# Inverses of a gated DeltaNet layer in eight rows of products, and weight casts placed behind the layer's first norms

## The chip, the cores and the metric

The kernel runs on one core of a Trainium2 chip. The metric is the device time of one execution in microseconds; the time before is the median of three runs. The profile is of one execution, taken by the hardware profiler. TensorE (PE) does the matrix products and loads its weights beside them (PEld); VectorE (DVE), ScalarE (ACT) and GpSimd (POOL) do the rest; SyncE (SP) issues most transfers.

## The reference

A trunk of two residual layers works on 512 tokens of width 1024. Layer 0 mixes tokens by gated linear attention, layer 1 by a gated DeltaNet, and a gated ConvFFN follows each; every sublayer ends in a LayerNorm. What the change touches lies in layer 1:

```python
# DeltaNet, in chunks, per head
m = where(strict, einsum('bhnik,bhnjk->bhnij', k_beta, k) * decay_ij, 0.0)
rhs = concatenate([v * beta, k_beta * exp(bcum)], -1)
sol = triangular_solve(m, rhs, lower=True, unit_diagonal=True)
u, w = split(sol)
# then a scan over the chunks: v_new = u - w @ state; o = (q*exp(bcum)) @ state + qk @ v_new; ...
y = (rms_norm(o) * silu(gate)) @ w_out
h = layer_norm(ALPHA * h + y, ln_g[i, 0], ln_b[i, 0])
# ConvFFN
g, up = split(causal_dwconv(h @ w_in, conv_w))
h = layer_norm(ALPHA * h + (gelu(g) * up) @ w_out, ...)
```

Instead of the solve, the kernel forms the inverse of the unit triangular matrix, for eight heads and four chunks of 128 tokens.

## The kernel before

All wide products are done in three terms: each operand is split into a high part (a cast by ScalarE) and the rest (a subtraction by VectorE), both at reduced precision (`split_out`, L728), and high by high, high by low and low by high are summed in PSUM. Weights come in tiles of 128x1024: a load on SP's queue into one of three raw buffers (`RAWB`), then the cast `wh` and the subtraction `wl` into one of four pairs (`WB`). `prefetch` issues these tiles ahead of their use, in the order of a plan that is written beforehand (`plan_fm` for feature tiles, `plan_tm`, `plan_fold` and `plan_gated` for the others); `look` says how many tiles ahead, and `held` counts those that hold a pair.

The order of the work is written by a small planner in Python: `clk` is its estimate of PE's time, `spawn` starts a side task after a delay, `flags` say when something will be ready, and `pump` lets the side tasks whose time has come emit their instructions between two stretches of wide products. The tile framework then schedules these instructions by their order and its own estimates. Up to the first mixer's input products the order of PE is pinned (`keep_in_program_order`); from there on it isn't (`self.pin = False`). `behind(a, b)` adds an edge that keeps a behind b in the schedule.

**The inverses** (`inverses` in `gdn`). Blocks of 32x32 are inverted on VectorE (`base`) and reach PE's operands by DRAM: `rm` is the inverse that is being filled, `T` (`t8`) holds its diagonal blocks transposed, `am` is the matrix itself. Two heads make a pair, so there are four pairs. The doubling from 32 to 64 (`quarter(k)`) and from 64 to 128 (`half(k)`) has two products each: V = am times T, copied from PSUM, and then R from V and rm, copied into `rm`. A step k does the V of pair k and the R of pair k-1, for the eight (head, chunk) units of the pair. There are ten steps, five of each kind. Before each, `block_turn(INV_APART)` waits for its time and places the first product of the row behind the last 512-column product. Full inverses set the flag `("rm", head)`, for which the chains over the chunks (`chain(0)` for heads 0 to 3, `chain(1)` for 4 to 7) wait. Meanwhile PE works on the last feature tiles of the input products (`fm`) and on the gate's products (`gated`, tile name `fold`), which hold four PSUM banks of eight.

**The output projection and the norm** (`mixer_out`, `out_proj`, `ln`). The output is made in two halves of 512 columns. For the second half (`last`) all eight 128x512 weight pieces wait in slots (`wsh`, `wsl`), and the four token blocks of 128 are done one after the other: products, update of the residual `h` (L625), statistics (L632), and `ln` is spawned for the block. Its first part aggregates the statistics (L880), takes the root, and normalises the two halves of the block: ScalarE one (L903), VectorE the other (L904). Its second part transposes them on PE (`xT`, L234), applies gain and bias on ScalarE (L917), and splits them into the operand `xh`, `xl` of the feed-forward (L921, L924, L925). A third part makes the residual on POOL (L941, L942). `look` is raised to 8 at the start of the second half, so the first four feature tiles of the feed-forward are issued there, before the first block's products. `fm_items` then takes the first four feature tiles for tokens 0 to 255 first, as soon as blocks 0 and 1 are there, and for the other tokens later.

Of the kernel before, what the change touches and what calls it, by code (L numbers as in the profile page):

```python
# [13 lines left out]
ALU = mybir.AluOpType  # L14
# [5 lines left out]
NC = D // P  # L20
# [31 lines left out]
RAWB = 3  # L52
WB = 4
LOOKAHEAD = 2
TAIL = 4
HEADSTART = 4
HALVES = {True: 3, False: 4}
# [21 lines left out]
class Trunk:  # L79
# [3 lines left out]
    def __init__(self, ctx, tc):  # L83
        self.tc = tc
        self.nc = nc = tc.nc
        self.n = 0
        ec = ctx.enter_context
        ap = ec(tc.tile_pool(name="acts", bufs=1))
        self.xh = ap.tile([P, NC, S], F32R, name="xh", tag="xh")
        self.xl = ap.tile([P, NC, S], F32R, name="xl", tag="xl")  # L90
        self.wp = ec(tc.tile_pool(name="wts", bufs=WB))
        self.hp = ec(tc.tile_pool(name="resid", bufs=2 * NTB))
        self.rp = ec(tc.tile_pool(name="raws", bufs=RAWB))
        self.cp = ec(tc.tile_pool(name="const", bufs=1))
        self.sp = ec(tc.tile_pool(name="small", bufs=4))
        self.pp = ec(tc.tile_pool(name="ps", bufs=8, space=bass.MemoryType.PSUM))
        self.dp = ec(tc.tile_pool(name="scratch", bufs=1, space=bass.MemoryType.DRAM))
        self.mp = None
        self.stage("gla", GLA_SLOTS)
        self.resets()  # L100
        self.ident = self.keep([P, P], "ident")
        ones = self.keep([P, 32], "one")
        self.one, self.warm, self.eps = (ones[:, i:i + 1] for i in range(3))
        nc.gpsimd.memset(ones, 1.0)
        make_identity(nc, self.ident)
        nc.gpsimd.memset(self.eps, LN_EPS)
        self.h = None
        self.plan = []
        self.issued = 0
        self.loaded = 0  # L110
        self.taken = 0
        self.held = 0
        self.look = 1
        self.pin = True
        self.ready = []
        self.dve = 0.0
        self.clk = 0.0
        self.tasks = []
        self.flags = {}
        self.tabled = None  # L120
        self.wide = None
        self.block = None
        self.traced = None
        self.spilled = False
        self.next_block = 0.0
        self.parts = []
        self.after = ()
        self.inverted = {}
        self.third = None
        self.first = None  # L130
        self.pieces = []
        self.late = []
# [346 lines left out]
    def prefetch(self):  # L479
        while self.issued < min(len(self.plan), self.taken + self.look):  # L480
            self.load_ahead(self.issued + 1)
            item = self.plan[self.issued]
            if self.held == WB and not self.in_slots(item):
                break
            if self.issued >= self.taken and self.flags.get(("split", *item[2:4]), 0.0) > self.clk:
                break
            self.ready.append(self.issue(item))
            self.issued += 1
        self.load_ahead(self.taken + self.look + AHEAD)
# [123 lines left out]
                else:  # L613
                    done(tb, ps[tb][piece], piece, blk(piece, S // m))

    def out_proj(self, a, n, first, final, pieces=1):

        nc = self.nc
        self.st = [None] * NTB
        for hf in range(2):  # L620
            def done(tb, ps, piece=None, cols=slice(0, S), hf=hf):
                h, ps = self.h[tb][hf][:, cols], ps[:, cols]
                if first:
                    self.wait(("h", tb, hf))
                    nc.vector.scalar_tensor_tensor(h, h, ALPHA, ps, ALU.mult, ALU.add)  # L625
                else:
                    nc.vector.tensor_add(h, h, ps)
                self.vec(0.7, self.clk + 0.4)
                if final is not None:
                    if hf == 0:  # L630
                        self.st[tb] = self.small([P, 1 + (pieces if tb == NTB - 1 else 1), 6], f"ln_st{pieces}")
                    nc.vector.bn_stats(self.st[tb][:, hf + (piece or 0), :], h)  # L632
                    self.vec(0.7)
                    if hf == 1 and piece in (None, pieces - 1):
                        self.spawn(final(tb))
                        self.pump()

            last = hf == 1 and final is not None
            if last:
                self.sqrt_table()  # L640
                self.look = TAIL + WB
            self.tm_half(a, n, TAIL if last else 1, done, last, pieces if last else 1)
        self.look = LOOKAHEAD


    def out_rows(self, a, n, final, pieces):
# [7 lines left out]
        for tb in range(NTB):  # L654
# [29 lines left out]
            self.pump()  # L684
        self.look = LOOKAHEAD

# [101 lines left out]
    def load_x(self, x):  # L788
# [34 lines left out]
        def arrive(i):  # L823
            self.opening(*self.x_part(i, 1))
            self.opening(*split(2 * i + 1))
            if i:
                self.look = 1
                self.prefetch()
                for tb in range(2, NTB):
                    for hf in range(2):  # L830
                        load(tb, hf)
                self.look = LOOKAHEAD
                self.prefetch()
# [60 lines left out]
    def ln(self, tb, spill=False):  # L894

        nc = self.nc
        li, h = self.li, self.h[tb]
        for hf in range(2):
            self.flags.pop(("h", tb, hf))
        mv, rs = self.ln_stats(tb)  # L900
        nb = self.small([P, 1], "ln_nb")
        nc.vector.scalar_tensor_tensor(nb, mv[:, 0:1], -1.0, rs, ALU.mult, ALU.mult)
        nc.scalar.activation(h[1], h[1], AF.Identity, bias=nb, scale=rs)  # L903
        nc.vector.tensor_scalar(h[0], h[0], mv[:, 0:1], rs, op0=ALU.subtract, op1=ALU.mult)  # L904
        ready = self.vec(0.65)
        yield ready - self.clk + 0.2
        for hf in range(2):
            ps = self.psum("xT")
            self.tr4(ps, h[hf])
            xf = self.slot("xf")  # L910
            for j in range(4):
                c = li * NC + 4 * hf + j
                if spill and hf and tb == NTB - 1:
                    nc.vector.tensor_scalar(xf[:, blk(j)], ps[:, blk(j)], self.lg[:, c:c + 1], self.lb[:, c:c + 1],
                                            op0=ALU.mult, op1=ALU.add)
                else:
                    nc.scalar.activation(xf[:, blk(j)], ps[:, blk(j)], AF.Identity,  # L917
                                         bias=self.lb[:, c:c + 1], scale=self.lg[:, c:c + 1])
            xs = (slice(None), slice(4 * hf, 4 * hf + 4), blk(tb))
            if hf == 0:  # L920
                nc.vector.tensor_copy(self.xh[xs], c4(xf))  # L921
                self.vec(0.42, self.clk + 1.8)
            else:
                nc.scalar.copy(self.xh[xs], c4(xf))  # L924
            nc.vector.tensor_sub(self.xl[xs], c4(xf), self.xh[xs])  # L925
            ready = self.vec(0.7, self.clk + (2.6 if hf else 0.0))
        self.set(("x", tb), max(0.1, ready - self.clk))
        yield 0.0

        self.spilled = spill  # L930
        if spill:
            for hf in range(2):
                nc.gpsimd.dma_start(self.hd[blk(tb), blk(hf, S)], h[hf])
            self.h[tb] = None
            return
        for i in range(NTB):
            yield from self.until(("x", i))
        yield RESID_DELAY + 10.0 * tb
        gb = self.ln_gb()
        for hf in range(2):  # L940
            nc.gpsimd.tensor_mul(h[hf], h[hf], gb[hf])  # L941
            nc.gpsimd.tensor_add(h[hf], h[hf], gb[2 + hf])  # L942
            self.set(("h", tb, hf))
            yield 5.0
# [153 lines left out]
    def folded(self, forms, first):  # L1098
# [25 lines left out]
        for name, _, form, at in FOLD:  # L1124
            f = FORMS.index(form) * 256
            for i in range(0, m, 2):
# [13 lines left out]
                self.spend()  # L1140
        self.look = LOOKAHEAD

# [114 lines left out]
    def gated(self, forms, tag, done, last):  # L1257
# [45 lines left out]
        for name, form, at in GATED:  # L1303
# [31 lines left out]
            if last:  # L1335
                forms.pop(form, None)
        self.look = LOOKAHEAD


    def gla_plan(self, w_in, w_out):  # L1340
# [6 lines left out]
        self.plan_gated(w_in, 2048)  # L1347
        self.plan_out(w_out, 0, NC, TAIL)

# [237 lines left out]
        self.gated(forms, "sg", gate_done, True)  # L1587
        self.mixer_out(y, li, g, b)

    def mixer_out(self, y, li, g, b, final=None):  # L1590
        self.ln_begin(li, g, b)

        def a(c, tb):
            hf = c // 4
            self.wait(("y", tb, hf))
            return tuple(t[:, blk(c % 4)] for t in y[tb][hf])

        self.out_proj(a, NC, True, self.ln)


    def gdn_plan(self, w_in, w_out):
# [35 lines left out]
    def gdn(self, li, g, b):  # L1637
        nc = self.nc
# [11 lines left out]
        q, k, v, am, rm, pj = ([None] * DH for _ in range(6))  # L1650
# [177 lines left out]
        def inverses():  # L1828
# [63 lines left out]
                        self.set(("rm", 2 * k - 2 + i), 1.0)  # L1892
                    parts[k - 1] = views[k - 1] = None

            for step, k in ((quarter, 0), (quarter, 1), (quarter, 2), (half, 0), (quarter, 3), (half, 1), (quarter, 4),
                            (half, 2), (half, 3), (half, 4)):
                yield from self.block_turn(INV_APART)
                step(k)
                yield 0.1

        vc = [None, None]
# [38 lines left out]
        y = [[None, None] for _ in range(NTB)]  # L1940
# [113 lines left out]
        self.gated(forms, "sg", gate_done, True)  # L2054
        self.wait(("r2", 1))
        self.unspill(spilled)
        self.mixer_out(y, li, g, b)


@with_exitstack  # L2060
# [73 lines left out]
```

## Time and profile before

| | us |
|---|---|
| median of three runs | 1217.04 (1217.03 to 1218.46) |
| the profiled execution, its own time | 1218.18 |
| its span, first to last instruction | 1216.5 |
| PE busy | 1209.2 |
| VectorE busy | 924.2 |
| ScalarE busy | 628.7 |

The inverses run from 711.7 to 746.8 us of the span, the second half of layer 1's output projection from some 832 to 856, and the last feed-forward from there to the end. The granted clock of TensorE is 0.999. In a timeline row stand the start, the duration, the engine, the line, the operation, output and inputs by name, shapes and count; in brackets the idle time before it and what ended it. Matmuls overlap in the pipeline, so their pace is read from start to start and not from the durations.

### The profile page before, as it was taken

To read this page: it belongs to the slowest core of one execution; us is meant where nothing else is said; L and a number is where in the kernel's file an instruction comes from. 1 tells how busy PE (TensorE), PEld (TensorE's weight loads), DVE (VectorE), ACT (ScalarE), POOL (GpSimd) and SP (SyncE) were. 2 spreads that over 40 slices of the span, in tenths; PEclk is the share of its full clock that TensorE was granted. 3 is DMA by queue.
4 is the path that set the end of the run, shared out by engine and by line. 5 is a ranking of instruction groups with operands and counts; after the bars stand their busy time and mean duration, and the time that the engine had idled before them with its cause. 6 is when DMAs were issued, how large, how long until landed. Compare 5 with 4: busy or idle time off the path is not lost.

```text
span 1216.5 us, 17219 instructions
## 1 busy us (share of the span) xinstructions
PE 1209.2 (99%) x6477; PEld 1020.5 (84%) x6477; DVE 924.2 (76%) x1527; ACT 628.7 (52%) x1116; POOL 172.3 (14%) x211
## 2 busy tenths in 40 slices
PE   9999999999999999999999999999999999999998
PEld 8888888988888888889888888988988888888886
DVE  6989778687757675766789969798697757775667
ACT  5666664644434443444678557863644433443440
POOL 3030101601100110001242032200610100020000
PEclk9999999999999999999999999999999999999999
DMA  8384642535743554433444356445434853383311
GB/s 233 109 164 114 142 150 76 188 108 129 194 126 88 122 104 121 118 108 90 110 127 130 102 133 108 109 134 157 145 115 108 184 159 103 104 174 89 111 61 70
DMA packets 177907, 152.55 MB, mean 125 GB/s; under 512 B 16966, under 2 KB 140938, under 8 KB 177824
## 3 DMA queue, kind: packets, MB, share of 16 engines
q1 hardware_dynamic: 161920, 115.23, 32.0%
q0 software_dynamic: 14944, 35.57, 15.3%
q8 instruction: 51, 0.84, 0.3%
q10 hardware_dynamic: 960, 0.66, 0.2%
q14 instruction: 32, 0.26, 0.1%
HBM read 133.06 MB, written 5.78 MB: 114 GB/s over the span
## 4 chain that ended last, share of the span: by engine, by line
PE 91%; DVE 5%; DMA 2%; issue 1%; ACT 1%; POOL 0%; SPq 0%; DVEq 0%; ACTq 0%; POOLq 0%
PE fm L216 51%; PE fold L216 21%; PE tm L216 10%; PE o L216 1%; PE xT L234 1%; DVE wl L728 1%; DVE conv L1632 1%; DVE tmp L1792 1%; PE pg L216 1%; PE yT L234 1%; DVE tt L1794 1%; PE V L216 0%; DMA h<-hd 0%; PE ds L216 0%; PE vn L216 0%
## 5 line engine op out<-in xcount | busy, mean ns | idle before, releaser
L216 PE MATMUL fm<-xh,wh 128*128 128x512 f32 (+2 forms) x1096 | 400.3, 368 | 0.7 <-ACT xh L728 0.7
L216 PE MATMUL fm<-xl,wh 128*128 128x512 f32 (+2 forms) x1096 | 398.7, 366 | 0.0
L216 PE MATMUL fm<-xh,wl 128*128 128x512 f32 (+1 forms) x1072 | 391.4, 367 | 0.0
L728 DVE TENSOR_TENSOR wl<-raw,wh 128x1024 fp32r<-128x1024 f32 (+1 forms) x156 | 193.6, 1243 | 142.9 <-ACT wh L728 142.8
L728 ACT CAST wh<-raw 128x1024 fp32r<-128x1024 f32 (+1 forms) x157 | 162.7, 1038 | 206.4 <-PE fm L216 131.9
L216 PEld LDWEIGHTS fm<-xh,wh 128*128 128x128 f32 (+1 forms) x1096 | 205.4, 188 | 34.2 <-ACT xh L728 1.0
L216 PEld LDWEIGHTS fm<-xl,wh 128*128 128x128 f32 (+1 forms) x1096 | 205.4, 188 | 33.0 <-DVE xl L925 0.2
L216 PEld LDWEIGHTS fm<-xh,wl 128*128 128x128 f32 x1072 | 201.2, 188 | 33.3
L1031 DVE SCALAR_TENSOR_TENSOR conv<-fm,ffn_cw,conv 128x511 f32<-128x511 f32 x112 | 83.5, 745 | 9.2 <-ACT conv L1029 7.5
L728 ACT CAST wh<-b 128x1024 fp32r<-128x1024 f32 x48 | 50.2, 1054 | 74.0 <-PE fold L216 34.0
L216 PE MATMUL fold<-wh,fh 128*128 128x512 f32 x224 | 87.6, 391 | 0.0
L216 PE MATMUL fold<-wh,fl 128*128 128x512 f32 x224 | 87.2, 389 | 0.0
L216 PE MATMUL fold<-wl,fh 128*128 128x512 f32 x224 | 87.2, 389 | 0.0
L728 DVE TENSOR_TENSOR wl<-b,wh 128x1024 fp32r<-128x1024 f32 x48 | 58.3, 1222 | 22.5 <-ACT wh L728 22.0
L415 POOL DMA_DIRECT2D b<-b x24 | 20.8, 914 | 353.3 <-DVE wl L728 309.8
L1049 ACT ACTIVATE conv<-conv 128x512 f32<-128x512 f32 x44 | 27.8, 632 | 64.2 <-DVE conv L1031 64.2
L1632 DVE SCALAR_TENSOR_TENSOR conv<-fm,gdn_cw,conv 128x511 f32<-128x511 f32 (+2 forms) x72 | 54.0, 789 | 8.1 <-ACT conv L1630 7.5
L216 PEld LDWEIGHTS fold<-wh,fh 128*128 128x128 f32 x224 | 42.0, 188 | 9.6 <-DVE h L1120 1.0
L216 PEld LDWEIGHTS fold<-wh,fl 128*128 128x128 f32 x224 | 42.0, 188 | 8.8
L216 PEld LDWEIGHTS fold<-wl,fh 128*128 128x128 f32 x224 | 42.1, 188 | 8.7
L1031 DVE SCALAR_TENSOR_TENSOR form<-fm,ffn_cw,form 128x511 f32<-128x511 f32 x64 | 47.7, 746 | 1.1
L941 POOL TENSOR_TENSOR h<-h,gb 128x512 f32<-128x512 f32 x16 | 24.7, 1567 | 132.9 <-PE xT L234 71.5
(362 smaller groups left out, 2058.1 us busy)
## 6 DMA issues: line engine op xcount, KB each, us to landing
raw<-in_ffn_w_in_dram SPq DMA_DIRECT2D x88, 512.0 KB, 3.8
raw<-in_gdn_w_in_dram SPq DMA_DIRECT2D x28, 512.0 KB, 4.1
b<-in_ffn_w_out_dram SPq DMA_DIRECT2D x24, 512.0 KB, 6.1
b<-b POOLq DMA_DIRECT2D x24, 512.0 KB, 4.6
raw<-in_ffn_w_out_dram SPq DMA_DIRECT2D x20, 512.0 KB, 3.8
raw<-in_gla_w_in_dram SPq DMA_DIRECT2D x18, 512.0 KB, 4.0
gw<-in_gla_w_in_dram POOLq DMA_DIRECT2D x8, 512.0 KB, 7.0
raw<-in_gla_w_out_dram SPq DMA_DIRECT2D x8, 512.0 KB, 3.7
```

The source lines that it names most:

```text
L216: t = self.nc.tensor.matmul(out, a, b, start=start, stop=stop, skip_group_check=joined)
L234: t = self.nc.tensor.transpose(out, a, self.ident[:n, :n])
L415: self.nc.gpsimd.dma_start(out, group[src, i][:, cols], accum_op=ALU.add)
L728: return self.nc.scalar.copy(dst_h, src), self.nc.vector.tensor_sub(dst_l, src, dst_h)
L941: nc.gpsimd.tensor_mul(h[hf], h[hf], gb[hf])
L1031: nc.vector.scalar_tensor_tensor(a[:, d:], ps[:, :S - d], tap(2 - d), a[:, d:], ALU.mult, ALU.add)
L1049: nc.scalar.activation(a, a, AF.Gelu)
L1632: self.conv = nc.vector.scalar_tensor_tensor(a[:, d:], ps[:, :S - d], tap(3 - d), a[:, d:], ALU.mult, ALU.add)
L1792: nc.vector.tensor_tensor(tv, m3[:, j, j + 1:].unsqueeze(2).to_broadcast([P, n, m]), t3[:, j, :m].unsqueeze(1).to_broadcast([P, n, m]), AL ...
L1794: nc.vector.tensor_add(t3[:, j + 1:, :m], t3[:, j + 1:, :m], tv)
```

## The change

The ten steps of the inverses come in eight turns: `quarter(2)` and `half(0)` share one, and so do `quarter(4)` and `half(2)`. Their order is the same. And in `mixer_out` of the DeltaNet layer alone (`late`), `prefetch` issues no feature tile while the second half of the output projection begins; when block 0's norm has been spawned it issues two, with the subtraction of each placed behind that block's L904, and after block 1's norm the others, behind block 1's L904. The cast on ScalarE gets no such edge.

```diff
@@ prefetch
+            if item[0] == "fm" and self.issued - self.held_from >= self.allowed:
+                break
@@ out_proj
                         self.spawn(final(tb))
                         self.pump()
+                        if late and tb < 2:
+                            self.allowed, self.after = (2, NO_LIMIT)[tb], (None, self.normed)
+                            self.prefetch()
+                            self.after = ()
             last = hf == 1 and final is not None
             if last:
+                if late:
+                    self.held_from = next(i for i in range(self.issued, len(self.plan)) if self.plan[i][0] == "fm")
+                    self.allowed = 0
                 self.sqrt_table()
                 self.look = TAIL + WB
@@ ln
-        nc.vector.tensor_scalar(h[0], h[0], mv[:, 0:1], rs, op0=ALU.subtract, op1=ALU.mult)
+        self.normed = nc.vector.tensor_scalar(h[0], h[0], mv[:, 0:1], rs, op0=ALU.subtract, op1=ALU.mult)
@@ inverses
-            for step, k in ((quarter, 0), (quarter, 1), (quarter, 2), (half, 0), (quarter, 3), (half, 1), (quarter, 4),
-                            (half, 2), (half, 3), (half, 4)):
+            for steps in (((quarter, 0),), ((quarter, 1),), ((quarter, 2), (half, 0)), ((quarter, 3),), ((half, 1),),
+                          ((quarter, 4), (half, 2)), ((half, 3),), ((half, 4),)):
                 yield from self.block_turn(INV_APART)
-                step(k)
+                for step, k in steps:
+                    step(k)
                 yield 0.1
@@ gdn
-        self.mixer_out(y, li, g, b)
+        self.mixer_out(y, li, g, b, True)
```

More of the change, by code (lines that the diff above doesn't have):

```diff
@@ L54 @@
 LOOKAHEAD = 2
+NO_LIMIT = 1 << 20
 TAIL = 4
@@ L128, in __init__ @@
         self.inverted = {}
+        self.held_from, self.allowed = 0, NO_LIMIT
         self.third = None
@@ L614, in tm_half, with out_proj @@
                     done(tb, ps[tb][piece], piece, blk(piece, S // m))
-    def out_proj(self, a, n, first, final, pieces=1):
+    def out_proj(self, a, n, first, final, pieces=1, late=False):
         nc = self.nc
@@ L1588, in gla, with mixer_out @@
         self.mixer_out(y, li, g, b)
-    def mixer_out(self, y, li, g, b, final=None):
+    def mixer_out(self, y, li, g, b, late=False):
         self.ln_begin(li, g, b)
@@ L1596, in a @@
             return tuple(t[:, blk(c % 4)] for t in y[tb][hf])
-        self.out_proj(a, NC, True, self.ln)
+        self.out_proj(a, NC, True, self.ln, late=late)
     def gdn_plan(self, w_in, w_out):
```

## The prediction

> **What bounds the kernel now.** I read the page first, then the waits of TensorE (PE), then the timeline of the two places that the diff touches.
>
> ```profile
> span 1216.5 us, 17219 instructions
> ## 1 busy us (share of the span) xinstructions
> PE 1209.2 (99%) x6477; PEld 1020.5 (84%) x6477; DVE 924.2 (76%) x1527; ACT 628.7 (52%) x1116; POOL 172.3 (14%) x211
> ```
>
> TensorE is busy for 1209.2 of 1216.5 us. A busy PE is not a PE at its peak, so the waits alone don't settle what could be won; but they say where it stands still:
>
> ```profile
> PE warm L810 <- POOL one L104: 1.0, 1, 1.0
> PE fm L216 <- ACT xh L728: 0.7, 1, 0.7
> PE mid L216 <- ACT diag L957: 0.6, 1, 0.6
> PE xT L234 <- DVE ln_rs L888: 0.5, 1, 0.5
> PE V L216 <- DMA T<-dinvt: 0.3, 1, 0.3
> ```
>
> That is the whole list, 3.1 us. The first two are the start of the program and the third its end; the diff reaches neither. What it can reach are the last two and the slow steps at which a matmul begins later than the one before it allows. Neither part removes or adds an instruction on any engine: the same products, copies, casts and loads are put in another order. So the sum is one of steps and stalls on PE, and both signs are small.
>
> **Part one, the joined rows.** A row of products of the inverses stands between two stretches of wide (512-column) products. This is PE's timeline around the third row (quarter step 2):
>
> ```profile
> 719.12 0.39 PE L216 MATMUL fm<-xh,wl 128*128 128x512 f32 x1
> 719.44 0.21 PE L216 MATMUL V<-T,am 32*32 32x32 f32 x1
> ...
> 720.49 0.50 PE L216 MATMUL fm<-xh,wh 128*128 128x512 f32 x1
> 720.83 0.39 PE L216 MATMUL fm<-xl,wh 128*128 128x512 f32 x1
> 721.06 0.40 PE L216 MATMUL fm<-xh,wl 128*128 128x512 f32 x1
> ```
>
> From start to start a wide product takes 0.23 us (720.83 to 721.06). Into the row the step is 0.32 (719.12 to 719.44), 0.09 too long. Out of it the first wide one takes 0.34 (720.49 to 720.83), 0.11 too long. A join takes one way out and one way in off PE: 0.20 us, or 0.40 for two joins. What it puts in their place is a change from 32x32 to 64x64 products inside the row, which this trace does not show. From below it costs nothing; from above as much as a way into a row, 0.09. I take the lower end, because the way out, which touches the wide weights, is the dearer half and goes altogether. So **-0.4 us**, with -0.2 as the other end if each change costs 0.09.
>
> By the Trainium skill, page "TensorEngine Tiling (Array Packing)", section "Key Properties", it is the change of tiling mode that drains TensorE. Counted so, two rows with a wide stretch between them have four changes and a joined row three, and the gain would be a quarter of the four ways (0.10 us for each join, 0.20 for both). The 0.09 at 719.44 agrees with such a drain; no run here shows yet what 32x32 to 64x64 costs.
>
> A join also asks for more at once: the row takes its PSUM banks together. In the gate's products four banks hold the sums; quarter step 4 takes two and half step 2 two more, which is all eight. The step before it, half step 1, is read out late:
>
> ```profile
> 729.51 0.22 PE L216 MATMUL R<-rm,V 64*64 64x64 f32 x1
> ...
> 732.74 0.41 DVE L1886 COPY rm<-R 64x256 f32<-64x256 f32 x1
> ```
>
> Its last product starts at 729.51 and the copy that frees its bank ends at 733.15, 3.6 us on. The next row now comes after one wide stretch of six (1.38 us) and its own way in. If the order keeps the row there, PE could wait up to 3.6 - 1.4 = 2.2 us. I take nothing, since the order of PE from here on isn't pinned and other wide products can be put ahead; +2.2 is the bound. The same holds for what follows: inverses end two stretches earlier (2 x 1.38 + 0.4, some 3.2 us), the head chains begin as much earlier, and the wide products that stood between come later. That moves work and takes none away.
>
> **Part two, the casts behind the norms.** In the second half of the output projection, DVE does this:
>
> ```profile
> 836.49 1.22 DVE L728 TENSOR_TENSOR wl<-raw,wh 128x1024 fp32r<-128x1024 f32 x1
> ...
> 838.83 1.28 DVE L1000 TENSOR_TENSOR h<-h,gb 128x512 f32<-128x512 f32 x2
> 840.03 0.68 DVE L625 SCALAR_TENSOR_TENSOR h<-h,tm 128x512 f32<-128x512 f32 x1
> 841.52 1.23 DVE L728 TENSOR_TENSOR wl<-raw,wh 128x1024 fp32r<-128x1024 f32 x1 [0.81 <-ACT wh L728]
> 842.67 0.69 DVE L632 BATCH_NORM_STATS2 ln_st<-h 128x6 f32<-128x512 f32 x1
> 843.34 1.23 DVE L728 TENSOR_TENSOR wl<-raw,wh 128x1024 fp32r<-128x1024 f32 x1
> 844.48 0.20 DVE L880 BATCH_NORM_AGGREGATE ln_mv<-ln_st 128x2 f32<-128x12 f32 x1
> ...
> 846.39 0.54 DVE L904 TENSOR_SCALAR h<-h,ln_mv,ln_rs 128x512 f32<-128x512 f32 x1
> ```
>
> The update of token block 0 (840.03), its statistics (842.67) and their aggregate (844.48) stand in line with casts of the feed-forward's weights: two ahead of the update, the later of them at 836.49, and two between update and aggregate (841.52 and 843.34). The normalised block (L904) is done at 846.93. And this is PE there:
>
> ```profile
> 846.22 0.39 PE L216 MATMUL tm<-wsl,yh 128*128 128x512 f32 x1
> 847.08 1.06 PE L234 MATMUL xT<-ident,h 128*128 128x128 f32 x8 [0.47 <-DVE ln_rs L888]
> ```
>
> The step is 0.86 instead of 0.23: **0.63 us** lost. With the change all four casts come behind L904 of block 0 or 1. Between update and aggregate that frees two casts and the 0.81 us that the first of them waited, 0.81 + 2 x 1.23 = 3.3 us, where 0.63 is wanted; what the two earlier casts leave comes on top. I take the whole 0.63; the other end is nothing (a rival below).
>
> What is late next: the four casts, 4 x 1.23 = 4.9 us, now stand between block 0's norm and the first products of the feed-forward. There DVE and PE read:
>
> ```profile
> 849.92 0.43 DVE L921 CAST xh<-xf 128x512 fp32r<-128x512 f32 x1 [1.81 <-ACT xf L917]
> ...
> 857.53 0.68 DVE L925 TENSOR_TENSOR xl<-xf,xh 128x512 fp32r<-128x512 f32 x1
> ```
>
> ```profile
> 857.92 0.28 PE L216 MATMUL fm<-xh,wl 128*128 128x256 f32 x1
> 858.04 0.28 PE L216 MATMUL fm<-xh,wh 128*128 128x256 f32 x1
> 858.26 0.38 PE L216 MATMUL fm<-xl,wh 128*128 128x256 f32 x1
> ```
>
> PE already waits here for the low part of block 1, which DVE ends at 858.21: a step of 0.22 where 0.12 is due. So DVE has no slack in this stretch but 1.81 us of idling at 849.92. Against the 4.9 us stand that idling and the 3.3 us by which the norm is earlier, together 5.1. The cover is just enough. I count the step at 858.04 as unchanged, from -0.1 (gone) up to the price of the slower rival.
>
> The queues: an edge puts the DVE half of each cast behind L904 on the same engine, so it adds no wait of its own there, and behind the casts stand the updates and evictions of the next blocks. The ScalarE half has no edge, but there are three raw buffers: the fourth tile's load can be issued on SP's queue only when the first cast has let its buffer go, and ScalarE's cast waits for that load with the root and the evictions of the next blocks behind it. Such a load takes
>
> ```profile
> raw<-in_ffn_w_in_dram SPq DMA_DIRECT2D x7, 512.0 KB, 4.3
> ```
>
> 4.3 us. With L904 at some 843.6 (3.3 earlier), the first cast is over at 844.9, the load lands at 849.2 and that cast is done by 851.6, before PE's first feed-forward products near 857. The norm's gain and bias loads stand behind on SP and come some microseconds later, so do POOL's multiplications:
>
> ```profile
> 851.26 6.14 POOL L941 TENSOR_TENSOR h<-h,gb 128x512 f32<-128x512 f32 x4 [60.27 <-DMA gb<-in_ln_g_dram]
> ```
>
> They make residuals that are read at the first folded products, after 16 more feature tiles; that costs nothing.
>
> **The sum.** -0.4 for the rows, -0.63 for the transposes, 0 for the rest: -1.0 us. The profiled run took 1218.18 us by its own time with a span of 1216.5; it would become 1217.1 with a span of 1215.5. The median of the runs before is 1217.04, so the forecast is **1216.0 us**.
>
> **Rivals.**
> *Fewer switches (faster).* The head chains start earlier and the two halves of heads meet otherwise. In the chain of waits, a stretch of six wide products takes
>
> ```profile
> 742.60 1.59 PE fold L216 x6
> ...
> 770.43 1.39 PE fold L216 x6
> ```
>
> 1.59 after a row of inverses and 1.39 after a row of the chains, so a stretch that ends up beside no row saves 0.2 us. If eight stretches fall out of the interplay of rows and chains, that is -1.6 on top: 1214.4 us. For it: the two joins are the only rows that go for certain, and the order is made anew from there on. Against it: each chain's steps are set apart by waits of their own, so their number stays.
>
> *The stall moves along.* The order on PE is fitted to a plan, so the transposes may be placed earlier by as much as the norm is and be late again by the same 0.6; the joins cost 0.09 each. Then -0.2: 1216.8 us. For it: PE stood waiting at 846.22 though other products were ready. Against it: the planner's error came with DVE's queue of casts, and that is gone.
>
> *DVE late at the feed-forward (slower).* The place is block 1's low part. It decides from the point where block 0's norm is no earlier than now. Then L904 ends at 846.93, the first cast at 848.2, the fourth tile's load lands at 852.5, and DVE has 4.9 us more to do before 858.21 with 1.81 us of idling to pay for it: 3.1 us late, all of it on PE. With -0.4 for the rows: 1219.7 us. For it: DVE has no other slack there. Against it: 0.81 + 2.46 us leave the norm's own path.
>
> *POOL holds DVE (a rule).* If POOL's multiplications stay where they are and casts fall among them, two casts wait for one each, 6.14 / 4 = 1.5 us: +3.1 on the forecast, 1219.1 us. It hangs on the Trainium skill, page "SBUF — State Buffer", section "Who interferes with whom": a DVE instruction with two SBUF inputs and a GpSimd one that reads SBUF block each other in full; the casts' subtraction is of that kind. Against it: POOL's gain loads come later too.
>
> **How the numbers follow.** A measurement of this kernel tells some 0.2% (2.4 us) from no change. Forecast 0.40; stall moves along 0.22; fewer switches 0.20; DVE late 0.13; POOL 0.05. Only the fewer switches reach below 1214.6: faster 0.20. Above 1219.5 lies DVE late, and a wait for banks of 2.2 us with one of the slower cases: slower 0.14. The rest, 0.66, is the same. The forecast's own bounds are narrow, 1215.9 to 1216.2. The range goes from 1213.8, below the faster rival's figure, to 1219.8, past the slower one's.
>
> **What would show it.** Right: no wait of the xT transposes for DVE left among PE's waits; eight rows of V and R products; PE's step at the first feed-forward products still near 0.12; PE busy within 1 us of now in a span of about 1215.5. Wrong: a wait of PE for xl (L925), for copies of R (L1886, L1866) or for the feed-forward's wl; a change from 32x32 to 64x64 over 0.2 us; or the span shorter by more than the two places give, which would mean that the order elsewhere has changed.

## The result and the profile after

| | before | after |
|---|---|---|
| median | 1217.14 us (5 runs) | 1227.08 us (5 runs, 1225.81 to 1227.51) |
| profiled execution, own time | 1218.18 us | 1227.51 us |
| span | 1216.5 us | 1225.8 us |

The ratio is 1.0075 with a 95% interval of 1.0064 to 1.0086: the change makes the kernel 9.9 us slower by the medians (7.8 to 10.5 by the interval), where the forecast was 1216.0 and the range ended at 1219.8. Of the kernels in the experiments below, one execution of rows_only (2469 us) and one of gate_before (1759 us), in both cases the traced one, took far longer than the others of the same kernel, and both are left out of the medians. The head of the page of after:

```profile
span 1225.8 us, 17207 instructions
## 1 busy us (share of the span) xinstructions
PE 1212.6 (99%) x6477; PEld 1024.5 (84%) x6477; DVE 928.0 (76%) x1527; ACT 628.7 (51%) x1116; POOL 170.0 (14%) x211
```

The work is the same, 6477 products and 1527 VectorE instructions; PE is busy 3.4 us longer and idle for longer too. TensorE's waits in after:

```profile
PE xT L236 <- DVE h L915: 3.7, 1, 3.7
PE pq L218 <- ACT vn L1979: 2.4, 1, 2.4
PE warm L821 <- POOL one L105: 1.0, 1, 1.0
PE fm L218 <- ACT xh L739: 0.7, 1, 0.7
```

Two long waits are new: 2.4 us among the inverses and the head chains, and 3.7 us before the last transposes of the norm (lines have moved: L236 was L234, L915 was L904). The wait for block 0's norm is gone from the list. The same two places by stretches (busy time of each engine, then the granted clock, the DMA share and GB/s):

```profile
738.00:741.50 3.50, 1.06 (x10) 0.87 (x8) 1.69 (x2) 2.74 (x7) 0.16 (x1) 1.00 0.55 100
741.50:746.30 4.80, 4.80 (x26) 4.66 (x26) 1.51 (x3) 4.74 (x23) 1.02 (x1) 0.64 0.60 83
746.30:750.00 3.70, 3.70 (x33) 3.25 (x33) 3.45 (x7) 2.98 (x11) 0.00 (x0) 1.00 0.21 38
868.90:872.80 3.90, 0.28 (x3) 0.07 (x1) 3.87 (x4) 0.81 (x1) 3.90 (x4) 0.95 0.39 145
872.80:876.00 3.20, 3.17 (x16) 3.17 (x17) 0.48 (x1) 2.02 (x6) 3.20 (x3) 0.53 0.00 0
```

Behind each wait the mean granted clock falls, to 0.64 over 4.8 us and to 0.53 over 3.2 us. That is another (1 - 0.64) x 4.8 = 1.7 us and (1 - 0.53) x 3.2 = 1.5 us. So the two places cost 2.4 + 1.7 = 4.1 and 3.7 + 1.5 = 5.2 us. In narrower stretches the means turn out to be one stretch of half clock each, 3.41 us long; the first begins only 1.2 us after PE has gone on at 741.49:

```profile
739.06:741.49 2.43, 0.00 (x1) 0.00 (x1) 1.68 (x2) 2.40 (x7) 0.15 (x1) 1.00 0.31 56
742.72:746.13 3.41, 3.41 (x17) 3.31 (x16) 1.34 (x2) 3.37 (x19) 0.00 (x0) 0.50 0.79 108
872.42:875.84 3.42, 3.01 (x14) 3.01 (x15) 0.68 (x2) 1.86 (x6) 3.42 (x4) 0.50 0.00 0
```

By the Trainium skill, page "TensorE: Matmul & The Clock Gate", section "Part 1: The HAM clock gate (the "warmup" mystery)", TensorE falls back to half its clock after an idle window of some 3.4 us. The half agrees with the 0.50 here; the window does not, since 2.43 us of idle time were enough.

That 4.1 and 5.2 add up to the 9.3 us by which the spans differ is in part chance. From the first product of the inverses (at 711.67 before, 711.08 after) to the first of the output projection (808.25, 813.27) the kernel loses 5.6 us, 1.5 more than the first place costs; from there to the first folded product of the last feed-forward (946.93, 956.28) it loses 4.3, 0.9 less than the second place costs, since the stall of 0.63 us at block 0 is gone; and it was 0.6 us ahead when the inverses began.

**The first place.** ScalarE in after, with the idle time before each instruction and its releaser in brackets:

```profile
731.65 0.58 ACT L1894 COPY V<-V 64x512 f32<-64x512 f32 x1 [0.70 <-PE V L218]
738.74 1.04 ACT L739 CAST wh<-gw 128x1024 fp32r<-128x1024 f32 x1 [6.50 <-DMA gw<-in_gdn_w_in_dram]
739.81 0.58 ACT L1289 COPY sg<-fold 128x512 f32<-128x512 f32 x1
740.29 1.15 ACT L1979 ACTIVATE vn<-vn,gd_bp 128x128 f32<-128x128 f32 x4
```

and the same work before:

```profile
738.63 0.58 ACT L1883 COPY V<-V 64x512 f32<-64x512 f32 x1 [0.68 <-PE R L216]
739.24 0.59 ACT L1278 COPY sg<-fold 128x512 f32<-128x512 f32 x1
739.72 1.05 ACT L728 CAST wh<-gw 128x1024 fp32r<-128x1024 f32 x1
741.12 1.14 ACT L1967 ACTIVATE vn<-vn,gd_bp 128x128 f32<-128x128 f32 x4 [0.35 <-PE vn L216]
```

The copy at the top is that of half step 2. The cast that follows is the first of the gate's third quarter (`t1`), and `issue_gated` places it behind that very copy: `zip(parts, self.inverted[2 + i // 2])`. The join brought half step 2 from 738.63 to 731.65, 7.0 us, and the cast with it. What the cast reads is summed by two loads, and the second was there only at 738.7. So ScalarE stood before the cast for 6.50 us, and in its queue behind it stood the copy of a gate sum and the evictions of the head chains. PE's `pq` products, which waited for the eviction `vn`, don't read it; that they waited for the PSUM bank that it freed is argued from this.

**The second place.** VectorE in after, the norms of blocks 2 and 3 from the aggregate (L891) to the normalised half (L915):

```profile
857.77 0.21 DVE L891 BATCH_NORM_AGGREGATE ln_mv<-ln_st 128x2 f32<-128x12 f32 x1
...
859.07 0.54 DVE L915 TENSOR_SCALAR h<-h,ln_mv,ln_rs 128x512 f32<-128x512 f32 x1
...
863.83 0.21 DVE L891 BATCH_NORM_AGGREGATE ln_mv<-ln_st 128x2 f32<-128x12 f32 x1
...
867.25 1.06 DVE L900 SCALAR_TENSOR_TENSOR ln_t<-ln_rs,ln_var 128x1 f32<-128x1 f32 x1
868.34 1.21 DVE L901 SCALAR_TENSOR_TENSOR ln_rs<-ln_t,ln_rs 128x1 f32<-128x1 f32 x1
...
870.07 1.21 DVE L913 SCALAR_TENSOR_TENSOR ln_nb<-ln_mv,ln_rs 128x1 f32<-128x1 f32 x1
871.21 1.57 DVE L915 TENSOR_SCALAR h<-h,ln_mv,ln_rs 128x512 f32<-128x512 f32 x1
```

Block 2 takes 1.8 us for this, block 3 takes 8.9. Three of block 3's five steps on a single column last 1.06 to 1.21 us; in block 2 the same three took 0.16 to 0.22. POOL, meanwhile:

```profile
863.86 5.68 POOL L952 TENSOR_TENSOR h<-h,gb 128x512 f32<-128x512 f32 x4 [71.95 <-DVE ln_st L636]
869.49 5.64 POOL L953 TENSOR_TENSOR h<-h,gb 128x512 f32<-128x512 f32 x4
```

Before, POOL did four of these from 851.26 and then waited for the bias to be loaded; now eight run without a break from 863.86 to 875.13, over the whole of block 3's norm. They start later because the gain is loaded later, behind the feed-forward's tiles on SP, whose raw buffers the moved casts release later (before, then after).

```profile
845.05 1.48 SPq L867 DMA_DIRECT2D gb<-in_ln_g_dram  x2
```

```profile
857.40 1.68 SPq L878 DMA_DIRECT2D gb<-in_ln_g_dram  x2
```

The loads issued from 857.40 on take 5.7 to 6.7 us to land, so POOL could not begin before 863.1; POOL's row names the statistics that ended at 863.80 as the last thing it waited for.

### The profile page after: what moved, and what is told of

Same layout as the page of the kernel before. It is cut to its first block, busy times and chain, and to the rows that moved or that the text cites. A ratio compares the mean times of both kernels' runs of the same rounds, so it can differ in the third digit from the quotient of the medians.

```text
span 1225.8 us, 17207 instructions
## 1 busy us (share of the span) xinstructions
PE 1212.6 (99%) x6477; PEld 1024.5 (84%) x6477; DVE 928.0 (76%) x1527; ACT 628.7 (51%) x1116; POOL 170.0 (14%) x211
## 4 chain that ended last, share of the span: by engine, by line
PE 85%; DVE 7%; ACT 3%; DMA 2%; issue 2%; SPq 1%; POOL 0%; DVEq 0%; ACTq 0%; POOLq 0%
PE fm L218 47%; PE fold L218 21%; PE tm L218 10%; PE o L218 2%; DVE conv L1643 2%; DVE wl L739 2%; PE xT L236 1%; DMA gw<-in_gdn_w_in_dram 1%; ACT dt L1707 1%; DVE tmp L1803 1%; DMA raw<-in_ffn_w_in_dram 1%; DVE tt L1805 1%; PE yT L236 1%; PE s L218 1%; PE vn L218 1%
## 5 line engine op out<-in xcount | busy, mean ns | idle before, releaser
L218 PE MATMUL fold<-wh,xh 128*128 128x512 f32 x104 | 43.0, 414 | 0.3 <-DVE sg L1307 0.2
```

The costliest lines, as they stand in the source:

```text
L218: t = self.nc.tensor.matmul(out, a, b, start=start, stop=stop, skip_group_check=joined)
```

## The experiments

The two parts were first taken apart, then each suspected cause was taken away alone. Medians of one set are compared with the kernel before as it ran beside them.

| kernel | median us | before | ratio, 95% interval |
|---|---|---|---|
| rows_only | 1222.65 | 1217.93 | 1.0043 (1.0028 to 1.0058) |
| casts_only | 1219.64 | 1217.93 | 1.0015 (1.0005 to 1.0024) |
| rows_anchor | 1219.59 | 1217.93 | 1.0014 (1.0005 to 1.0023) |
| casts_gate | 1221.90 | 1217.93 | 1.0034 (1.0021 to 1.0046) |
| join1 | 1217.87 | 1217.76 | 1.0002 (0.9993 to 1.0011) |
| join2 | 1217.83 | 1217.76 | 1.0002 (0.9993 to 1.0011) |
| anchor_early | 1220.82 | 1217.76 | 1.0025 (1.0016 to 1.0034) |
| casts_gate2 | 1217.41 | 1217.76 | 0.9998 (0.9989 to 1.0007) |
| after_gate | 1222.87 | 1217.82 | 1.0038 (1.0025 to 1.0052) |
| after_anchor | 1223.65 | 1217.82 | 1.0049 (1.0035 to 1.0062) |
| both_mended | 1218.55 | 1217.82 | 1.0008 (0.9999 to 1.0016) |
| gate_before | 1217.51 | 1217.82 | 0.9997 (0.9988 to 1.0006) |

**rows_only**: the kernel before with the eight turns of the change, and nothing of the casts.

> The joined rows alone, casts as before. Theory: PE's stall at 738.8 us of the changed kernel (2.6 us, pq waiting for vn on ScalarE) and the lower granted clock behind it (0.64 over 4.8 us, 1.7 us) belong to this part, less 0.4 to 0.6 us of saved ways in and out: 1217.1 + 4.3 - 0.5 = 1220.9. ScalarE's cast wh<-gw waits some 6.5 us for its load here too. Rival: the stall needs the other part as well, or belongs to it: 1216.7.

4.7 us slower (3.4 to 7.1 by the interval), where 3.8 were expected (1217.1 to 1220.9); the two can't be told apart. The loss belongs to the rows by themselves. That ScalarE's cast waits 6.5 us here too is not shown.

**casts_only**: the casts of the change, the ten turns of before.

> The casts behind the norms alone, ten rows as before. Theory: PE's stall at 868.9 (3.8 us, the transposes of token block 3 waiting for its norm) and the clock of 0.53 behind it (1.5 us) belong to this part, less the 0.6 us stall at block 0's transposes: 1217.1 + 5.3 - 0.6 = 1221.8. Rival: the place of the casts matters only with the rows joined: 1216.5.

1.7 us slower, where 4.7 were expected. The wait is there, but shorter:

```profile
PE xT L236 <- DVE h L915: 2.1, 2, 1.6
```

One wait of 1.6 us for block 3's norm and one of 0.5 for block 0's: the stall of 0.63 us at block 0's transposes, which the casts were to remove, is still there 4.5 us earlier (the transposes start at 842.62 instead of 847.08, the norm is done at 842.47 instead of 846.93). The granted clock stays 1.00 here. Block 3's norm itself is held almost as long as in after, 8.1 us (858.55 to 866.68) against 8.9; POOL begins 0.5 us after its aggregate here (859.03) and 0.03 us after it there. What differs more is the work that PE had left: it stops 6.5 us after the aggregate here and 5.3 in after. So the cost of POOL's place hangs on what PE still has to do beside it.

**rows_anchor**: the joined rows with a later edge for the casts of the third quarter.

```diff
-            for ins, other in zip(parts, self.inverted[2 + i // 2]):
+            for ins, other in zip(parts, self.inverted[3]):
```

> The joined rows alone, and both casts of the gate's third quarter (t1) placed behind the copies of half step 3 instead of half steps 2 and 3. Theory: the join moved half step 2, behind which the first of these casts stands, 7 us ahead of the load that the cast needs, so ScalarE stood 6.5 us in front of its queue; with the later anchor ScalarE's wait falls under 1.5 us, the stall of PE is gone and the time is 1217.1 - 0.5 = 1216.6. Rival: a joined row takes four to five PSUM banks at once and PE waits for banks whatever ScalarE's order: the stall stays, 1220.9 as with the rows alone.

This edit alone takes 1222.65 to 1219.59, 3.1 us. ScalarE now does the chains' evictions first and the cast when its load is there:

```profile
736.64 0.58 ACT L1883 COPY V<-V 64x512 f32<-64x512 f32 x1 [3.65 <-PE V L216]
737.25 0.59 ACT L1278 COPY sg<-fold 128x512 f32<-128x512 f32 x1
737.73 1.15 ACT L1968 ACTIVATE vn<-vn,gd_bp 128x128 f32<-128x128 f32 x4
...
743.51 1.10 ACT L728 CAST wh<-gw 128x1024 fp32r<-128x1024 f32 x1
```

The rival of the banks falls for the 2.4 us, which are gone from PE's waits. But 1.7 us of loss remain where a gain of 0.5 was expected. Part of it stands within the second joined row, where PE stops before one of half step 2's products:

```profile
731.01 0.28 PE L216 MATMUL V<-T,am 64*64 64x64 f32 x2
732.04 0.27 PE L216 MATMUL R<-rm,V 64*64 64x64 f32 x1 [0.75 <-issue]
```

The profile shows nothing that this product waited for.

**join1** and **join2**: one of the two joins each, nine turns.

```diff
 join1: ((quarter, 2), (half, 0)) joined, ((quarter, 4),), ((half, 2),) apart
 join2: ((quarter, 2),), ((half, 0),) apart, ((quarter, 4), (half, 2)) joined
```

> Only quarter step 2 and half step 0 joined (nine rows), casts as before. Theory: half step 2, behind which the cast for the gate's third quarter stands, comes one wide stretch (some 1.9 us) earlier, so ScalarE waits for the load some 2 us instead of 6.5; other reads of PSUM cover that and PE doesn't stop: 1217.9 - 0.2 = 1217.7, up to 1218.5 if the step within the row costs what the joined rows cost. Rival: the join itself stalls PE, half of the loss of both: 1220.5.

> Only quarter step 4 and half step 2 joined (nine rows), casts as before. Theory: half step 2 comes some 3 to 4 us earlier and ScalarE waits about 3 us for the load; PE's stall is under 1 us, its clock stays, and PE waits some 0.7 us within this row as it does with both joins: 1218.9. Rival: this join alone is the cause, whatever the load: 1222.5 or above.

Neither can be told from before, and neither brings its share of the gain. In join1 the cast waits for nothing (2 us were expected). In join2 ScalarE waits for the load of the third quarter for 1.8 us:

```profile
ACT wh L728 <- DMA gw<-in_gdn_w_in_dram: 1.8, 1, 1.8
```

and PE for nothing in this place: the work at hand covers 1.8 us. One join moves half step 2 by some 3 us (its copy starts at 735.09 and 735.78 instead of 738.63) and the cover holds; two joins move it by 7.0 and it doesn't.

**anchor_early**: no row is joined; only the edge is moved the other way.

```diff
+            for ins, other in zip(parts, self.inverted[1 + i // 2]):
```

> All ten rows as before, nothing joined; the first and second cast of the gate's third quarter are placed behind the copies of half steps 1 and 2 instead of 2 and 3. Theory: the first cast then stands on ScalarE some 9 us ahead of its place before and waits 6 us or more for the load without any join; PE stalls 2 us or more for evictions behind it and may lose its clock: 1220.5 to 1223. Rival: without a joined row nothing happens on PE: 1217.9.

3.1 us slower with the ten rows of before: an early edge costs time without any change to PE's rows. ScalarE's wait, then PE's:

```profile
ACT wh L728 <- DMA gw<-in_gdn_w_in_dram: 3.5, 1, 3.5
```

```profile
PE vn L216 <- DVE rm L1886: 2.2, 1, 2.2
```

ScalarE waits less than expected (3.5 us, not 6), and PE is stopped by VectorE's copy of an inverse, not by an eviction on ScalarE. The link is the other half of the moved pair, the subtraction `wl`: it waits for the late cast with VectorE's queue behind it, the copies of the inverse (L1886) start at 741.81 instead of 739.36, and PE waits for them:

```profile
738.69 1.23 DVE L728 TENSOR_TENSOR wl<-gw,wh 128x1024 fp32r<-128x1024 f32 x1 [2.94 <-ACT wh L728]
...
741.81 0.41 DVE L1886 COPY rm<-R 64x256 f32<-64x256 f32 x1
```

```profile
742.27 0.92 PE L216 MATMUL vn<-v,rm 128*128 128x128 f32 x4 [2.17 <-DVE rm L1886]
```

**casts_gate**: casts_only, and one small copy on POOL ahead of its multiplications, which is to make them wait for block 3's low part (in the trace one of them still runs ahead of the copy).

```diff
         gb = self.ln_gb()
+        if li == 2 and tb == 0:
+            nc.gpsimd.tensor_copy(self.small([P, 1], "ln_gate"), self.xl[:, NC - 1, S - 1:S].bitcast(F32))
```

> The casts alone, ten rows as before, and one 128x1 copy on POOL of the last column of block 3's low part ahead of POOL's multiplications of the residual, so that these start only when all norms of this place are done. Theory: POOL's eight operations in a row (863.9 to 875.1 us in the changed kernel) hold VectorE's steps of block 3's norm, 8.9 us from aggregate to end against 1.8 for block 2; without them block 3's norm takes 2 us, PE's stall is gone: 1217.1 - 0.7 = 1216.4. Rival: the 4.9 us of casts put VectorE behind in any case, so block 3's norm is late by 2.4 us or more and PE waits: 1219.5 or above.

The wait for block 3's norm is gone (block 0's, 0.7 us, is left), and yet the kernel is 4 us slower. It loses the time in stages that the edit doesn't touch: in the folded products of the feed-forward of layer 0, PE's 30 us from 300 to 330 hold 131 products, and 134 before (casts_gate, then before):

```profile
300.00:330.00 30.00, 30.00 (x131) 1.00 0.80 184
```

```profile
300.00:330.00 30.00, 30.00 (x134) 1.00 0.82 193
```

The only thing that the edit changes there is a new tile of one column in four buffers, by which later tiles may lie at other addresses.

**casts_gate2**: the same copy into a column that exists.

```diff
+            nc.gpsimd.tensor_copy(self.warm, self.xl[:, NC - 1, S - 1:S].bitcast(F32))
```

> The casts alone, ten rows as before, and the copy on POOL that holds its multiplications back, this time into a column that exists already, so that no tile is added and no address moves. Theory: the products before and after this place run at 0.2267 us again as in the kernel before, not at 0.232, and what is left is the place itself: PE's wait for block 3's norm gone, block 0's still there: 1217.9 - 0.3 = 1217.6. Rival: the slower pace has to do with the copy on POOL and not with the added tile: 1221.9 again.

1217.41 us, and 134 products in those 30 us. So the added tile cost 4.5 us, and POOL's place costs what the casts alone lost: 1.7 us slower than the kernel beside it becomes 0.35 faster. Of the promised 0.7 us some 0.35 are left, which can't be told from nothing.

**after_gate**, **after_anchor**, **both_mended**: the whole change with the copy of casts_gate2, with the edge of rows_anchor, and with both.

> The whole change, with POOL's multiplications held back by the copy into an existing column; the casts of the gate's third quarter stand as the change puts them. Theory: block 3's norm no longer runs beside POOL, so the stall of 3.8 us and the slower clock behind it (1.5 us) go, the loss at the inverses stays: 1227.1 - 5.3 = 1221.8. Rival: block 3's norm is late because the whole stretch is late, 1226 or above.

> The whole change, with both casts of the gate's third quarter behind half step 3; POOL as the change has it. Theory: the loss at the inverses shrinks by what the same edit gave with the rows alone (5.4 to 1.7, 3.7 us): 1227.1 - 3.7 = 1223.4, or 1221 if POOL's operations then fall on block 3's norm as in the casts alone and not as in the whole change (2 us). Rival: the edit does nothing beside the casts, 1227.

> The whole change with both repairs. Theory: the rows with the later edge cost 1.7 us, the casts with POOL held back gain 0.3: 1217.8 + 1.4 = 1219.2. Rival: the two places are not independent and something of the 9 us comes back: 1221 or above.

The copy gives 4.2 us (1227.08 to 1222.87), the edge 3.4 (to 1223.65), both 8.5 (to 1218.55). The four executions of after_gate lie between 1220.29 and 1223.94, and the trace is of the fastest: there ScalarE waits 5.0 us for its load instead of 6.5 and PE 1.0 us instead of 2.4, without a lower clock behind it. In after_gate block 3's norm goes from aggregate to end in 3.2 us instead of 8.9:

```profile
861.56 0.21 DVE L891 BATCH_NORM_AGGREGATE ln_mv<-ln_st 128x2 f32<-128x12 f32 x1
...
864.27 0.54 DVE L915 TENSOR_SCALAR h<-h,ln_mv,ln_rs 128x512 f32<-128x512 f32 x1
```

and PE's waits in both_mended hold nothing of the two:

```profile
PE fold L218 <- DVE sg L1309: 0.3, 1, 0.3
PE V L218 <- DMA T<-dinvt: 0.3, 1, 0.3
PE xT L236 <- DMA h<-in_x_dram: 0.3, 1, 0.3
```

With the two causes gone the change is 0.7 us slower than before with an interval that reaches 1: it brings nothing.

The traces tell the two places apart. Of one execution each, this is what it takes longer than before from the first product of the inverses to the first of the output projection, and from there to the first folded product of the last feed-forward:

| kernel | inverses and chains, us | output projection to folded products, us |
|---|---|---|
| after | +5.6 | +4.3 |
| after_gate | +3.7 | -0.9 |
| after_anchor | +1.4 | +3.4 |
| both_mended | +1.4 | -0.9 |
| rows_anchor | +2.5 | 0.0 |
| anchor_early | +2.8 | -0.3 |
| casts_only | -0.1 | +2.0 |
| casts_gate2 | +0.1 | -0.1 |

In the whole change the copy takes 5.2 us out of the second place, as much as its wait and clock came to, and the edge 4.2 out of the first, where 4.1 were counted. What is left of the joined rows is a loss of 1.4 us and more; what is left of the casts is a gain of 0.9 beside the joined rows and of 0.1 without them.

**gate_before**: the kernel before with POOL's copy alone.

> The kernel before with nothing but POOL's multiplications held back. Theory: POOL ran beside block 1's operand there and PE waited 0.2 us for it; that goes: 1217.6, not to be told from 1217.8. Rival: the copy on POOL is worth something by itself, more than 1 us, and the casts had no part in the gain of the kernel with casts and copy.

No difference. Where POOL's operations fell before, they cost the kernel nothing that can be measured here, though they held VectorE there too (see the second step that failed).

## Why the prediction was wrong

*The joins, -0.4 us.* Not seen: join1 and join2 stand at +0.1 each with an interval of 1 us to either side. The change from 32x32 to 64x64 inside a row costs more than the end that was taken (nothing):

```profile
719.83 0.19 PE L218 MATMUL R<-rm,V 32*32 32x32 f32 x1
719.95 0.27 PE L218 MATMUL V<-T,am 64*64 64x64 f32 x1
```

The second starts 0.12 us after the first, where the 32x32 products of the row start 0.01 to 0.02 apart. That is 0.10 over the pitch, as much as a way in, and leaves some 0.1 us for a join; a row that stops for 0.75 us, as in rows_anchor, eats both joins. Nor did the ways go for certain, as the prediction had it. In after the rows are nine and not eight: half step 3 is cut in two, at 734.12 and 735.50, by products of a head chain, and quarter step 3 comes in two pieces, 48 products at 722.61 and 32 at 724.82, the second joined to half step 1. Counted over PE's timeline from the first row to the last, changes between 128, 64 and 32 are 20 in before, 20 in join1, 19 in join2 and 21 in after. So there was next to nothing to save, and the rival "fewer switches" found none. The step of 0.12 agrees with the other count that the prediction gave, by which a change of tiling mode drains TensorE (the Trainium skill, "TensorEngine Tiling (Array Packing)", section "Key Properties").

*"That moves work and takes none away."* This is the first step that failed; it stood at nothing in the sum and cost 2.4 us of waiting and 1.7 of clock. The prediction listed what follows the inverses, and missed what is tied to them: an edge from half step 2 to a cast on ScalarE, in `issue_gated`, a function that the diff doesn't touch. A step that comes 7 us earlier takes its followers along, while a load keeps its time. The bound of +2.2 us named the right resource, PSUM banks, at the wrong place: by the releaser that the profile names they were held by an eviction behind the cast, not by the joined row.

*The stall of 0.63 us at block 0.* In after it is gone; in casts_only 0.5 us of waiting for that norm remain, so there the rival "the stall moves along" came true, which had 0.22: norm and transposes both come 4.5 us earlier. Against the forecast of 0.63 us stand a gain of 0.9 in this place in both_mended and of 0.1 in casts_gate2.

*The cover for the four casts.* Held: block 1's low part isn't waited for in after, and the steps of the first feed-forward products are 0.12 us from 861.95 on. The slower rival was built on it and didn't occur.

*"They make residuals that are read at the first folded products ...; that costs nothing."* This is the second step that failed: it too stood at nothing and cost 3.7 us of waiting and 1.5 of clock. The prediction saw the gain's loads slip on SP's queue and POOL's multiplications with them, and asked only who reads their result, not whom they run beside. The rival "POOL holds DVE" had the mechanism and 0.05; it expected two casts of weights held for 1.5 us each, with POOL where it was, and it was six steps of block 3's norm and its neighbours, three of them of one column, that were held by a POOL that had moved. The size of it stood in the trace of before: beside POOL's four operations (851.26 to 857.40) block 2's norm takes 5.7 us from aggregate to end (853.04 to 858.74), and the cast of 0.43 us that the prediction shows at 849.92 takes 1.21:

```profile
853.34 1.21 DVE L921 CAST xh<-xf 128x512 fp32r<-128x512 f32 x1
...
856.36 1.06 DVE L889 SCALAR_TENSOR_TENSOR ln_t<-ln_rs,ln_var 128x1 f32<-128x1 f32 x1
```

*The clock.* No case had it. 3.2 us are the half clock behind the two stalls.

*What stays open*: why PE stops for 0.75 us within the joined row, and where the rest of the 1.4 us and more goes that the joined rows lose with the edge mended.

## What to carry to other kernels

Before a step is moved, look for everything that is ordered by it, in functions that the diff leaves alone too: an edge that kept a cast behind its load by way of a third instruction holds only while all three keep their distance. Work off the critical path costs something when it moves beside an engine that it holds up, so ask beside what it will run, not only who reads it. On a TensorE that is 99% busy count the clock behind a stall too: here a stall of 2.4 us cost 4.1 and one of 3.7 us cost 5.2.

## What the runs showed of the hardware that was not expected

- VectorE's scalar_tensor_tensor steps on a single column (128x1) take 1.06 to 1.21 us beside POOL's multiplications and 0.16 to 0.22 without. In after the three of block 3 end at 868.31, 869.55 and 871.28, operations of POOL at 868.29, 869.53 and 871.27. The reciprocal (0.15) and the tensor_scalar (0.14) on one column kept their time beside POOL. The Trainium skill, page "SBUF — State Buffer", section "Who interferes with whom", says that a VectorE instruction with two SBUF inputs and a GpSimd one that reads SBUF block each other in full. The three steps agree: each reads two columns. That so small an instruction is held for a whole operation of POOL is what these rows add. The normalised half (L915), with one wide input, took 1.57 us instead of 0.54 and isn't covered by that sentence.
- Idle times of PE of 2.4 us (pq in after), 3.7 us (xT in after) and 2.6 us (xT in after_anchor) were each followed by 3.4 us at a granted clock of 0.50; the 2.2 us in anchor_early and 1.6 us in casts_only were not, with 1.00 behind them.
- A new tile of one column in four buffers slowed products in stages that have nothing to do with it, from 134 to 131 in 30 us, and the kernel by 4.5 us (1221.90 in casts_gate against 1217.41 in casts_gate2). That it is the addresses is argued, not shown.
